# A decoder layer on one core: GpSimd's sums moved to VectorE, bias and memory loaded from the weights' queue, query copies made by DMA

## The chip, the core and the metric

The kernel runs on one core of one Trainium2 chip. The metric is device time in microseconds (us). Engines are named as in the profile: PE is TensorE (PEld its weight loads), DVE is VectorE, ACT is ScalarE, POOL is GpSimd, SP is SyncE, which computes nothing here and issues transfers.

## What is computed

One layer over 256 tokens of width 1024, all in float32: RMSNorm, a combined projection, two self-attention mixers (8 heads of MoBA attention, which with 256 tokens is plain causal attention, and 4 heads of differential attention), then cross-attention to 256 memory tokens, a SwiGLU and a final RMSNorm.

```python
h = rms_norm(x, mix_norm_g)
proj = h @ w_in                        # qa, ka, va, qb, kb, vb
oa = moba_attention(qa, ka, va, table_a)            # softmax(q k / 8 + bias) v, causal
ob = diff_attention(qb, kb, vb, table_b, lam, ...)  # (softmax_0 - lam * softmax_1) v
x = x + concat(rms_norm(oa), rms_norm(ob)) @ w_out
m = rms_norm(mem, mem_norm_g)
x = x + cross_attention(rms_norm(x) @ w_cq, m @ w_ck, m @ w_cv) @ w_co
x = x + (silu(rms_norm(x) @ w_gate) * (rms_norm(x) @ w_up)) @ w_down
return rms_norm(x)
```

## The kernel before

**Weights.** All weights pass as a stream of 65 chunks of 1 MB (`wdma`, L112, SP's queue, three buffers `wr`). Each chunk is converted in four parts (`wpart`): ACT writes the rounded high part `wh` (L135), DVE subtracts it to get the low part `wl` (L120). The subtraction of a part is put into DVE's stream only when the next part is recorded (`held`, `wflush`). A product then takes three matmuls, high x high, high x low, low x high: one step of `ws` (L276) is six matmuls of 256 columns over one k tile and two output tiles, one step of `as_` (L298) three of 512 columns.

**Order.** Each engine runs its own stream in order. The streams are written by a hand-made clock of slots: `run` calls `tick` after each PE step, `at(slot, fn)` and `later(n, fn)` put other work between two steps. A weight part is recorded about every second slot. In slots: chunk 1 (keys `ka0`) to 16, `qa1` to 24, `ka1` to 32, values `v_chunk(0)` to 48, `qb0` to 56, `kb0` to 64, `qb1` to 72, `kb1` to 80, `v_chunk(1)` to 96, then the memory's keys from w_ck.

**The opening.** x comes in five transfers, interleaved on SP's queue with the first weight chunk. `x_gain` multiplies by the norm's gain, `wf` (L342) multiplies the first chunk in plain float32 without a split, `x_split` makes the two halves of h (L267, L268), `squares` squares x on ACT (L324) and adds the squares up on POOL (L326). `x_rstd` sums over partitions by matmul (L333), takes the power on POOL (L246); `x_row` (L253) makes the row RX of it, which `qk_evac` (L372, L375) needs.

**Queries and keys.** A chunk holds four heads of 64 lanes. `q_high` writes the rounded queries twice per half of the partitions (L383, four ACT instructions per chunk: own half and the other), so that keys can stand with their high part in one half and their low part in the other (`k_high` L395 on ACT, `k_low` L400 on DVE; `q_low` is L389). `logits` (L435, L436) runs 4 slots apart for the first mixer, `p_t` (L458) transposes the exponentials six slots later. For the second mixer `diff_mix` (L480) joins two heads before its `p_t`.

**Memory tokens.** `mem_load` brings them by POOL's queue; `mem_squares` (ACT, sums on POOL L326), `mem_rstd`, `mem_row`, `mem_scale` (POOL, L572), `mem_split` (`split_g`: gain and rounding on ACT L261, subtraction on DVE L263).

Of the kernel before, what the change touches and what calls it, by code (L numbers as in the profile page):

```python
# [17 lines left out]
P = 128  # L18
# [44 lines left out]
def layer(ctx: ExitStack, tc: tile.TileContext, xt_d, stream, memT, gains, bias_d, diff_lambda, final_norm_g,  # L63
# [124 lines left out]
    for lo, hi in ((0, 1), (1, 2), (2, 4), (4, 6), (6, 8)):  # L188
        nc.sync.dma_start(xT[:, lo:hi], xt_d[:, lo:hi])
        (nc.sync if lo else nc.scalar).dma_start(w0[:, lo:hi], src[:, lo:hi])  # L190
# [33 lines left out]
    def lambda_dma():  # L224
        nc.gpsimd.dma_start(lp.rearrange("p a b -> p (a b)"),
                            bass.AP(tensor=diff_lambda.tensor, offset=diff_lambda.offset,
                                    ap=[[0, P], [1, 256]]))

    def bias_load(h0, n):
        t = mx.tile([P, n, 256], FT, name="bias", tag="bias", bufs=2)  # L230
        for h in range(n):
            bias[h0 + h] = t[:, h, :]
        nc.gpsimd.dma_start(t, bias_d[:, h0:h0 + n, :])
# [87 lines left out]
    def squares(sqt, src, j):  # L321

        ks = slice(2 * j, 2 * j + 2)
        nc.scalar.activation(sqt[:, ks, :], src[:, ks, :], AF.Square)  # L324
        if j:
            nc.gpsimd.tensor_tensor(sqt[:, 0:2, :], sqt[:, 0:2, :], sqt[:, ks, :], op=OP.add)  # L326
# [229 lines left out]
    def mem_load():  # L556
        nc.gpsimd.dma_start(memv, memT)
# [25 lines left out]
    at(14, x_row)  # L583
    at(46, load_lambda)
    at(10, bias_load, 0, 4)
    at(18, lambda_dma)
    at(20, bias_load, 4, 4)
    at(32, mem_load)
    at(45, bias_load, 8, 4)
    for i in range(8):  # L590
        at(28 + 4 * i, logits, i, i, f"qa{i // 4}", f"ka{i // 4}", i // 2 % 2, i % 2)
        at(34 + 4 * i, p_t, i)
        at((51, 52, 53, 54, 56, 59, 63, 67)[i], pv, i, 0, "a", 64)
    for j in range(4):
# [27 lines left out]
    for j in range(4):
        at((108, 112, 124, 127)[j], mix_t, j)
# [383 lines left out]
```

## Time and profile before

| what | value |
|---|---|
| time, median of 3 runs | 428.75 us (427.72 to 429.9) |
| the profiled execution | 430.01 us, span of its instructions 427.8 us |
| busy in the span | PE 97%, DVE 69%, ACT 59%, POOL 7% |
| moved by DMA | 74 MB, 173 GB/s in the mean |
| mean granted clock of TensorE | 0.994 of full speed |

The page's shares are means over the span: they don't tell the stages apart. A busy PE is not PE at its peak, since the ends of matmuls are modelled; a stage is read from its waits and from the start times of successive matmuls.

### The profile page before, as it was taken

Reading aid. Unit: us, or ns where it says so; the run is one execution under the profiler, and the core shown is the slowest. Engines: PE = TensorE matmul, PEld = TensorE weight load, DVE = VectorE, ACT = ScalarE, POOL = GpSimd, SP = SyncE. Lnnn points to the kernel's source line nnn. Section 1 sums busy time; section 2 is a strip of 40 time slices with the busy share of each in tenths; the row PEclk is TensorE's granted clock in tenths of the full one; section 3 lists DMA queues with packets and bytes.
Section 4 is the critical chain, followed back from the end, with each engine's and each line's share of the span. In section 5 each row is a group of like instructions: output and inputs, shape, how many; then the busy total and the mean of one; then the engine's idle time right before and its main releaser. Section 6 shows DMA issues by size and latency. Waiting matters only on the chain.

```text
span 427.8 us, 6928 instructions
## 1 busy us (share of the span) xinstructions
PE 414.5 (97%) x2677; PEld 375.0 (88%) x2677; DVE 294.0 (69%) x591; ACT 253.4 (59%) x542; POOL 27.9 (7%) x36
## 2 busy tenths in 40 slices
PE   7979999979999999999999999999999999999994
PEld 4879899969998889998888999999888888888883
DVE  3677747989568589476759868888776666544423
ACT  5568869598576555366546565556656655433322
POOL 3500035100010000000000100000000000000001
PEclk9989999999999999999999999999999999999999
DMA  7984552235527534434442555545753575555002
GB/s 225 378 296 161 190 193 100 98 98 199 198 100 278 191 113 144 161 107 190 137 159 98 198 213 186 184 159 205 286 196 110 196 284 198 196 193 190 11 2 98
DMA packets 13040, 73.99 MB, mean 173 GB/s; under 512 B 1584, under 2 KB 2864, under 8 KB 4944
## 3 DMA queue, kind: packets, MB, share of 16 engines
q1 hardware_dynamic: 11664, 69.74, 46.0%
q0 software_dynamic: 768, 3.28, 2.1%
q10 hardware_dynamic: 576, 0.54, 0.4%
q8 instruction: 21, 0.34, 0.3%
q14 instruction: 11, 0.09, 0.1%
HBM read 72.50 MB, written 1.05 MB: 172 GB/s over the span
## 4 chain that ended last, share of the span: by engine, by line
PE 86%; DVE 7%; ACT 3%; issue 2%; DMA 1%; POOL 0%; SPq 0%; POOLq 0%; DVEq 0%; ACTq 0%
PE acc L276 24%; PE y L298 13%; PE acc L298 9%; PE acc L284 9%; PE att L284 9%; PE att L276 5%; PE att L285 4%; PE acc L285 4%; DVE wl L120 2%; PE att L765 1%; PE oc L809 1%; DVE b L263 1%; ACT qs L383 1%; DMA xT<-in_xT_dram 1%; PE att L458 1%
## 5 line engine op out<-in xcount | busy, mean ns | idle before, releaser
L120 DVE TENSOR_TENSOR wl<-wr,wh 128x512 fp32r<-128x512 f32 x255 | 164.5, 691 | 36.0 <-ACT wh L135 35.8
L135 ACT ACTIVATE wh<-wr 128x512 fp32r<-128x512 f32 x255 | 144.1, 620 | 51.1 <-issue 22.6
L276 PE MATMUL acc<-b,wh 128*128 128x256 f32 x536 | 101.2, 289 | 0.0
L276 PEld LDWEIGHTS acc<-b,wh 128*128 128x128 f32 x536 | 84.4, 194 | 0.2
L276 PE MATMUL acc<-b,wl 128*128 128x256 f32 x268 | 76.7, 286 | 2.8 <-DVE wl L120 2.6
L276 PEld LDWEIGHTS acc<-b,wl 128*128 128x128 f32 x268 | 51.9, 194 | 3.2 <-DVE wl L120 3.2
L298 PE MATMUL y<-wh,b 128*128 128x512 f32 x152 | 49.0, 391 | 0.0
L298 PE MATMUL acc<-wh,b 128*128 128x512 f32 x128 | 40.5, 397 | 0.0
L284 PE MATMUL acc<-hs,wh 128*128 128x512 f32 x96 | 37.8, 393 | 0.0
L284 PE MATMUL att<-hs,wh 128*128 128x512 f32 x96 | 37.8, 393 | 0.0
L298 PE MATMUL y<-wl,b 128*128 128x512 f32 x88 | 34.2, 389 | 0.0
L298 PEld LDWEIGHTS y<-wh,b 128*128 128x128 f32 x152 | 28.5, 188 | 5.9
L285 PE MATMUL att<-hs,wl 128*128 128x256 f32 x96 | 27.2, 283 | 0.0
L285 PE MATMUL acc<-hs,wl 128*128 128x256 f32 x96 | 27.1, 283 | 0.0
L298 PEld LDWEIGHTS acc<-wh,b 128*128 128x128 f32 x128 | 22.6, 189 | 3.6
L298 PE MATMUL acc<-wl,b 128*128 128x512 f32 x64 | 25.1, 392 | 0.0
L276 PE MATMUL acc<-cHL,wh 128*128 128x256 f32 x128 | 23.3, 283 | 0.0
L276 PE MATMUL att<-b,wh 128*128 128x256 f32 x128 | 23.2, 283 | 0.0
L284 PEld LDWEIGHTS att<-hs,wh 128*128 128x128 f32 x96 | 18.0, 188 | 4.2
L284 PEld LDWEIGHTS acc<-hs,wh 128*128 128x128 f32 x96 | 18.0, 188 | 4.1
L276 PEld LDWEIGHTS att<-b,wh 128*128 128x128 f32 x128 | 20.0, 192 | 0.0
L450 ACT ACTIVATE e<-e,nm 128x128 f32<-128x128 f32 (+1 forms) x32 | 14.3, 447 | 9.5 <-DVE nm L441 9.5
(206 smaller groups left out, 723.5 us busy)
## 6 DMA issues: line engine op xcount, KB each, us to landing
wr<-in_stream_dram SPq DMA_DIRECT2D x62, 1024.0 KB, 4.8
wr<-in_stream_dram SPq DMA_DIRECT2D x7, 256.0 KB, 6.2
bias<-in_bias_dram POOLq DMA_DIRECT2D x3, 512.0 KB, 5.6
wr<-in_stream_dram SPq DMA_DIRECT2D x2, 512.0 KB, 7.1
b<-in_memT_dram POOLq DMA_DIRECT2D x1, 1024.0 KB, 8.3
xT<-in_xT_dram SPq DMA_DIRECT2D x3, 256.0 KB, 5.3
gfin<-in_final_norm_g_dram POOLq DMA_DIRECT2D x1, 512.0 KB, 6.0
out_dram<-z ACTq DMA_DIRECT2D x2, 192.0 KB, 2.0
```

Of the source, the lines that this page charges most:

```text
L120: eng.tensor_tensor(l, t, h, op=OP.subtract)
L135: nc.scalar.activation(h, t, AF.Copy)
L263: nc.vector.scalar_tensor_tensor(dL[:, k, :], srcs[:, a, :], g(gi + k), dH[:, k, :], op0=OP.mult, op1=OP.subtract)
L276: nc.tensor.matmul(o[:, c, :], m[:, k, cs], b[:, k, :], start=first and c == 0 and q == 0, stop=last and q == 2, skip_group_check=True)
L284: nc.tensor.matmul(o[c], h[:, k, cs], flat(a[:, k]), start=first, stop=last, skip_group_check=True)
L285: nc.tensor.matmul(o[c][:, 0:256], l[:, k, cs], a[:, k, 0, :], start=False, stop=last, skip_group_check=True)
L298: nc.tensor.matmul(o, m[:, ka, ts], b[:, kw, cs], start=start and q == 0, stop=stop and q == 2, skip_group_check=True)
L383: nc.scalar.activation(qs[to, :, r, :], d[half(r)], AF.Copy)
L450: nc.scalar.activation(e[:, cs], e[:, cs], AF.Exp, bias=nm[:, t:t + 1], scale=-1.0, accum_out=lsum[:, i, t:t + 1])
L458: nc.tensor.transpose(b[:, q * P:(q + 1) * P], e[:, q * P:(q + 1) * P], ident)
L765: nc.tensor.matmul(b[:, t, :], a[:, kt, t * P:(t + 1) * P], k[:, kt, :], start=n == 0, stop=n == 5)
L809: nc.tensor.matmul(o[:, dv, :], v[:, mt, cs], p_[:, mt, :], start=n == 0, stop=n == 5)
```

## The change

Sums and products leave POOL: `squares` only squares, `add_squares` adds on DVE; `mem_scale` becomes one DVE instruction per k tile that takes the gain along, and `mem_split` splits without gain. `q_high` makes two ACT copies per chunk, and the other two are transfers inside SBUF, issued by POOL (L387 of the changed kernel). The bias table, lambda and the memory tokens are loaded from SP's queue, behind weight chunks. The gain of x is taken by DVE for six k tiles instead of four; the third and fourth k tile of x and of the first weights come in transfers of their own. Slots move: RX by one, the evacuation of `qa0` by two and of `ka0` by three, the first mixer's attention by two, the memory's norm by three, the second mixer's last four logits by two and its `p_t` by three or four.

```diff
-    for lo, hi in ((0, 1), (1, 2), (2, 4), (4, 6), (6, 8)):
+    for lo, hi in ((0, 1), (1, 2), (2, 3), (3, 4), (4, 6), (6, 8)):
         nc.sync.dma_start(xT[:, lo:hi], xt_d[:, lo:hi])
...
     def lambda_dma():
-        nc.gpsimd.dma_start(lp.rearrange("p a b -> p (a b)"),
+        nc.sync.dma_start(lp.rearrange("p a b -> p (a b)"),
...
-        nc.gpsimd.dma_start(t, bias_d[:, h0:h0 + n, :])
+        nc.sync.dma_start(t, bias_d[:, h0:h0 + n, :])
...
     def x_gain(k):
-        if k % 2:
+        if k % 4:
             nc.vector.tensor_scalar(hF[:, k, :], xT[:, k, :], g(G_MIX + k), None, op0=OP.mult)
...
     def squares(sqt, src, j):
         ks = slice(2 * j, 2 * j + 2)
         nc.scalar.activation(sqt[:, ks, :], src[:, ks, :], AF.Square)
+    def add_squares(sqt, j):
+        ks = slice(2 * j, 2 * j + 2)
         if j:
-            nc.gpsimd.tensor_tensor(sqt[:, 0:2, :], sqt[:, 0:2, :], sqt[:, ks, :], op=OP.add)
+            nc.vector.tensor_tensor(sqt[:, 0:2, :], sqt[:, 0:2, :], sqt[:, ks, :], op=OP.add)
...
     def q_high(name, d):
         qs = mx.tile([P, 2, 2, 256], FR, name="qs", tag="qs", bufs=2)
         for r in range(2):
-            for to in (half(r), half(1 - r)):
-                nc.scalar.activation(qs[to, :, r, :], d[half(r)], AF.Copy)
+            nc.scalar.activation(qs[half(r), :, r, :], d[half(r)], AF.Copy)
+        for r in range(2):
+            nc.gpsimd.dma_start(qs[half(1 - r), :, r, :], qs[half(r), :, r, :])
...
     def mem_load():
-        nc.gpsimd.dma_start(memv, memT)
+        nc.sync.dma_start(memv, memT)
...
     def mem_squares(j):
         squares(mq, memv, j)
+        later(1, add_squares, mq, j)
...
-    def mem_scale(j):
-        t = memv[:, 2 * j:2 * j + 2, :]
-        nc.gpsimd.tensor_tensor(t, t, M["R"].to_broadcast([P, 2, 256]), op=OP.mult)
+    def mem_scale(k):
+        nc.vector.scalar_tensor_tensor(memv[:, k, :], memv[:, k, :], g(G_MEM + k), M["R"][:, 0, :], op0=OP.mult,
+                                       op1=OP.mult)
...
-        split_g(*m, j, memv[:, 2 * j:2 * j + 2, :], G_MEM)
+        ks = slice(2 * j, 2 * j + 2)
+        split(m[0][:, ks, :], m[1][:, ks, :], memv[:, ks, :])
...
-    at(14, x_row)
+    at(15, x_row)
...
-    at(18, lambda_dma)
-    at(20, bias_load, 4, 4)
-    at(32, mem_load)
-    at(45, bias_load, 8, 4)
+    at(26, lambda_dma)
+    at(28, bias_load, 4, 4)
+    at(38, mem_load)
+    at(47, bias_load, 8, 4)
...
-        at(28 + 4 * i, logits, i, i, f"qa{i // 4}", f"ka{i // 4}", i // 2 % 2, i % 2)
+        at(30 + 4 * i, logits, i, i, f"qa{i // 4}", f"ka{i // 4}", i // 2 % 2, i % 2)
...
-    at(59, mem_rstd)
-    at(62, mem_row)
+    at(62, mem_rstd)
+    at(64, mem_row)
...
-        at((73, 75, 77, 79, 88, 90, 92, 94)[i], logits, 8 + i, 8 + i // 2, f"qb{i // 4}", f"kb{i // 4}", i // 2 % 2,
+        at((73, 75, 77, 79, 90, 92, 94, 96)[i], logits, 8 + i, 8 + i // 2, f"qb{i // 4}", f"kb{i // 4}", i // 2 % 2,
...
-        at((78, 82, 93, 97)[hd], diff_mix, hd)
-        at((84, 88, 99, 101)[hd], p_t, 8 + 2 * hd)
+        at((79, 84, 96, 100)[hd], diff_mix, hd)
+        at((88, 92, 102, 104)[hd], p_t, 8 + 2 * hd)
...
-    later(7, qk_evac, o, "qa0", True)
+    later(9, qk_evac, o, "qa0", True)
...
-    later(1, qk_evac, o1, "ka0", False)
+    later(4, qk_evac, o1, "ka0", False)
```

Three places in the streams. Line numbers of the changed kernel are up to 14 higher. First DVE from the evacuation of `qa0` to the evacuation of `qa1`: `qa`, `ka` are evacuated projections, `wl` the low parts of weights, 64x2x256 the low parts of queries (`b<-qa,qs`) and keys. Before:

```order
L372 SCALAR_TENSOR_TENSOR qa_252<-acc,RX 128x512
L120 TENSOR_TENSOR wl<-wr,wh 128x512 x3
L389 TENSOR_TENSOR b_122<-qa_252,qs 64x2x256 x2
L375 TENSOR_TENSOR ka_281<-acc,RX 128x512
L400 TENSOR_TENSOR b_129<-ka_281,b_129 64x2x256 x2
L120 TENSOR_TENSOR wl<-wr,wh 128x512 x4
```

and changed:

```order
L375 SCALAR_TENSOR_TENSOR qa_274<-acc,RX 128x512
L393 TENSOR_TENSOR b_124<-qa_274,qs 64x2x256 x2
L120 TENSOR_TENSOR wl<-wr,wh 128x512
L378 TENSOR_TENSOR ka_306<-acc,RX 128x512
L120 TENSOR_TENSOR wl<-wr,wh 128x512
L404 TENSOR_TENSOR b_131<-ka_306,b_131 64x2x256 x2
L120 TENSOR_TENSOR wl<-wr,wh 128x512 x2
L375 SCALAR_TENSOR_TENSOR qa_350<-acc,RX 128x512
```

Four instructions on queries and keys stood in a row between the third and the fourth `wl` of the row behind `qa`; now a `wl` stands between the queries' two, the evacuation of `ka` and the keys' two.

Second POOL, behind its memsets. The first 12 rows before (`b_126`, `b_137` are squares, `b_136` the memory tokens):

```order
L326 TENSOR_TENSOR b_126<-b_126 128x512 x3
L233 DMA bias<-in_bias_dram 128x1024
L246 TENSOR_TENSOR rx<-rxv,mhalf 128x2
L225 DMA lp<-in_diff_lambda_dram 128x256
L233 DMA bias<-in_bias_dram 128x1024
L557 DMA b_136<-in_memT_dram 128x2048
L233 DMA bias<-in_bias_dram 128x1024
L326 TENSOR_TENSOR b_137<-b_137 128x512 x3
L246 TENSOR_TENSOR rm<-rmv,mhalf 128x2
L572 TENSOR_TENSOR b_136<-b_136,RM 128x512 x4
L246 TENSOR_TENSOR ra<-rav,mhalf 128x2
L246 TENSOR_TENSOR rb<-rbv,mhalf 128x8
```

and all that is left of them in the changed kernel:

```order
L246 TENSOR_TENSOR rx<-rxv,mhalf 128x2
L387 DMA qs<-qs 64x2x256 x6
L246 TENSOR_TENSOR rm<-rmv,mhalf 128x2
L387 DMA qs<-qs 64x2x256 x2
L246 TENSOR_TENSOR ra<-rav,mhalf 128x2
L246 TENSOR_TENSOR rb<-rbv,mhalf 128x8
```

The adds and products are gone, the loads too, and eight transfers of `qs` stand there, two per chunk of queries.

Third DVE from the evacuation of `kb0` to the second mixer's first logits (`b_136` and `b_138` are the memory tokens). Before:

```order
L375 TENSOR_TENSOR kb_835<-acc,RX 128x512
L120 TENSOR_TENSOR wl<-wr,wh 128x512
L263 SCALAR_TENSOR_TENSOR b_846<-b_136,gT,b_845 128x256 x2
L120 TENSOR_TENSOR wl<-wr,wh 128x512
L400 TENSOR_TENSOR b_129<-kb_835,b_129 64x2x256 x2
L263 SCALAR_TENSOR_TENSOR b_846<-b_136,gT,b_845 128x256 x2
L120 TENSOR_TENSOR wl<-wr,wh 128x512
L263 SCALAR_TENSOR_TENSOR b_846<-b_136,gT,b_845 128x256 x2
L120 TENSOR_TENSOR wl<-wr,wh 128x512
L263 SCALAR_TENSOR_TENSOR b_846<-b_136,gT,b_845 128x256 x2
L120 TENSOR_TENSOR wl<-wr,wh 128x512
```

and changed, from the first scaling on:

```order
L576 SCALAR_TENSOR_TENSOR b_138<-b_138,gT,RM 128x256 x2
L378 TENSOR_TENSOR kb_835<-acc,RX 128x512
L120 TENSOR_TENSOR wl<-wr,wh 128x512
L576 SCALAR_TENSOR_TENSOR b_138<-b_138,gT,RM 128x256 x2
L268 TENSOR_TENSOR b_848<-b_138,b_847 128x512
L120 TENSOR_TENSOR wl<-wr,wh 128x512
L576 SCALAR_TENSOR_TENSOR b_138<-b_138,gT,RM 128x256 x2
L404 TENSOR_TENSOR b_131<-kb_835,b_131 64x2x256 x2
L576 SCALAR_TENSOR_TENSOR b_138<-b_138,gT,RM 128x256 x2
L268 TENSOR_TENSOR b_848<-b_138,b_847 128x512
L120 TENSOR_TENSOR wl<-wr,wh 128x512
L268 TENSOR_TENSOR b_848<-b_138,b_847 128x512
```

Eight scalings (L576) have come in, and each pair of L263 has become one L268.

## Rows read from the trace of the kernel before

**Rows 1.** Part 1 of the page: busy time of each engine, share of the span, instructions.
```profile
PE 414.5 (97%) x2677; PEld 375.0 (88%) x2677; DVE 294.0 (69%) x591; ACT 253.4 (59%) x542; POOL 27.9 (7%) x36
```

**Rows 2.** Three stretches in the view of windows: the stretch and its length, then busy us (and instructions) of PE, PEld, DVE, ACT and POOL, the granted clock of TensorE as a share of full speed, the DMA engines' share and GB/s.
```profile
27.00:30.00 3.00, 0.60 (x6) 0.40 (x4) 2.18 (x4) 2.56 (x5) 0.00 (x0) 0.98 0.93 358
30.00:33.20 3.20, 2.97 (x14) 2.97 (x15) 2.58 (x5) 1.47 (x3) 0.00 (x0) 0.50 0.19 64
86.00:96.00 10.00, 7.71 (x37) 5.77 (x37) 9.15 (x26) 9.70 (x25) 0.00 (x0) 1.00 0.32 105
```

**Rows 3.** The view of waits, the rows of PE and its weight loads (PEld): who waited for whom, us in total, how often, the longest. The first three rows are of the whole span, the last two of its first 160 us.
```profile
PE acc L276 <- DVE wl L120: 2.6, 1, 2.6
PE att L458 <- DVE e L480: 1.2, 1, 1.2
PE att L435 <- DVE b L400: 1.0, 1, 1.0
...
PEld acc L276 <- DVE wl L120: 3.2, 2, 2.8
PEld pr L253 <- POOL rx L246: 0.3, 1, 0.3
```

**Rows 4.** PE in the timeline, at three restarts: start, us, engine, line, operation, operands, how many; in brackets the idle time before and what ended it.
```profile
30.23 0.58 PE L276 MATMUL acc<-b,wl 128*128 128x256 f32 x1 [2.63 <-DVE wl L120]
...
89.92 0.83 PE L458 MATMUL att<-ident,e 128*128 128x128 f32 x3 [1.19 <-DVE e L480]
...
94.51 0.33 PE L435 MATMUL att<-b,qs 128*128 128x128 f32 x1 [1.03 <-DVE b L400]
```

**Rows 5.** Three pieces of the chain that ended last: start, us, what, how many matmuls.
```profile
30.23 4.22 PE acc L276 x22
...
34.92 2.88 PE acc L276 x24
...
38.26 1.39 PE acc L298 x6
```

**Rows 6.** DVE in the timeline from 21 to 31 us, columns as in Rows 4.
```profile
21.23 1.29 DVE L120 TENSOR_TENSOR wl<-wr,wh 128x512 fp32r<-128x512 f32 x2
24.58 0.69 DVE L120 TENSOR_TENSOR wl<-wr,wh 128x512 fp32r<-128x512 f32 x1 [2.06 <-ACT wh L135]
25.19 1.38 DVE L389 TENSOR_TENSOR b<-qa,qs 64x512 fp32r<-64x512 f32 x2
26.61 0.69 DVE L375 TENSOR_TENSOR ka<-acc,RX 128x512 f32<-128x512 f32 x1
28.05 1.40 DVE L400 TENSOR_TENSOR b<-ka,b 64x512 fp32r<-64x512 f32 x2 [0.76 <-ACT b L395]
29.49 1.29 DVE L120 TENSOR_TENSOR wl<-wr,wh 128x512 fp32r<-128x512 f32 x2
```

**Rows 7.** ACT in the timeline over the same stretch.
```profile
21.35 2.56 ACT L383 ACTIVATE qs<-qa 64x512 fp32r<-64x512 f32 x4 [0.24 <-DVE qa L372]
23.92 1.15 ACT L135 ACTIVATE wh<-wr 128x512 fp32r<-128x512 f32 x2
27.39 1.28 ACT L395 ACTIVATE b<-ka 64x512 fp32r<-64x512 f32 x2 [2.32 <-DVE ka L375]
28.70 2.19 ACT L135 ACTIVATE wh<-wr 128x512 fp32r<-128x512 f32 x4
```

**Rows 8.** The opening in the timeline: one row of PE, two of DVE, one of POOL.
```profile
7.85 7.64 PE L342 MATMUL acc<-b,wr 128*128 128x256 f32 x32 [0.47 <-DMA wr<-in_stream_dram]
...
6.51 0.35 DVE L313 TENSOR_SCALAR b<-xT,gT 128x256 f32<-128x256 f32 x1
...
8.41 1.36 DVE L313 TENSOR_SCALAR b<-xT,gT 128x256 f32<-128x256 f32 x1
...
8.36 1.26 POOL L326 TENSOR_TENSOR b<-b 128x512 f32<-128x512 f32 x1 [4.59 <-ACT b L324]
```

**Rows 9.** The memory tokens and the second mixer in the timeline: one row of POOL, four of DVE, one of ACT.
```profile
70.53 5.68 POOL L572 TENSOR_TENSOR b<-b,RM 128x512 f32<-128x512 f32 x4 [1.90 <-ACT RM L255]
...
73.54 2.95 DVE L263 SCALAR_TENSOR_TENSOR b<-b,gT,b 128x256 fp32r<-128x256 f32 x2
...
79.96 0.87 DVE L263 SCALAR_TENSOR_TENSOR b<-b,gT,b 128x256 fp32r<-128x256 f32 x2
...
89.51 0.75 DVE L480 SCALAR_TENSOR_TENSOR e<-e,rl 128x128 f32<-128x128 f32 x2
...
93.77 1.41 DVE L400 TENSOR_TENSOR b<-kb,b 64x512 fp32r<-64x512 f32 x2
...
84.02 2.58 ACT L383 ACTIVATE qs<-qb 64x512 fp32r<-64x512 f32 x4
```

**Rows 10.** What a transfer costs: a DMA that POOL issues, and DVE at that time (timeline); then three rows of the view of transfers: tensors, queue, how many, KB each, median us from issue to landing.
```profile
46.37 0.54 POOL L233 DMA_DIRECT2D bias<-in_bias_dram  x1 [25.06 <-DVE nm L441]
...
45.99 0.69 DVE L120 TENSOR_TENSOR wl<-wr,wh 128x512 fp32r<-128x512 f32 x1
...
b<-in_memT_dram POOLq DMA_DIRECT2D x1, 1024.0 KB, 8.3
out_dram<-z SPq DMA_DIRECT2D x2, 128.0 KB, 1.9
lp<-in_diff_lambda_dram POOLq DMA_DIRECT2D x1, 128.0 KB, 5.5
```

More of the change, by code (lines that the diff above doesn't have):

```diff
@@ L224, in lambda_dma @@
     def lambda_dma():
-        nc.gpsimd.dma_start(lp.rearrange("p a b -> p (a b)"),
-                            bass.AP(tensor=diff_lambda.tensor, offset=diff_lambda.offset,
-                                    ap=[[0, P], [1, 256]]))
+        nc.sync.dma_start(lp.rearrange("p a b -> p (a b)"),
+                          bass.AP(tensor=diff_lambda.tensor, offset=diff_lambda.offset,
+                                  ap=[[0, P], [1, 256]]))
     def bias_load(h0, n):
@@ L578, in mem_split @@
             m.extend((slot(4), slot(5)))
-        split_g(*m, j, memv[:, 2 * j:2 * j + 2, :], G_MEM)
+        ks = slice(2 * j, 2 * j + 2)
+        split(m[0][:, ks, :], m[1][:, ks, :], memv[:, ks, :])
     at(12, x_rstd)
-    at(14, x_row)
+    at(15, x_row)
     at(46, load_lambda)
     at(10, bias_load, 0, 4)
-    at(18, lambda_dma)
-    at(20, bias_load, 4, 4)
-    at(32, mem_load)
-    at(45, bias_load, 8, 4)
+    at(26, lambda_dma)
+    at(28, bias_load, 4, 4)
+    at(38, mem_load)
+    at(47, bias_load, 8, 4)
     for i in range(8):
-        at(28 + 4 * i, logits, i, i, f"qa{i // 4}", f"ka{i // 4}", i // 2 % 2, i % 2)
-        at(34 + 4 * i, p_t, i)
-        at((51, 52, 53, 54, 56, 59, 63, 67)[i], pv, i, 0, "a", 64)
+        at(30 + 4 * i, logits, i, i, f"qa{i // 4}", f"ka{i // 4}", i // 2 % 2, i % 2)
+        at(36 + 4 * i, p_t, i)
+        at((53, 54, 55, 56, 58, 61, 65, 69)[i], pv, i, 0, "a", 64)
     for j in range(4):
-        at(52 + j, mem_squares, j)
-    at(59, mem_rstd)
-    at(62, mem_row)
+        at(57 + j, mem_squares, j)
+    at(62, mem_rstd)
+    at(64, mem_row)
+    for k in range(KT):
+        at(65 + k // 2, mem_scale, k)
     for j in range(4):
-        at(63, mem_scale, j)
         at((66, 68, 70, 72)[j], mem_split, j)
@@ L614, in layer @@
     for hd in range(4):
-        at((78, 82, 93, 97)[hd], diff_mix, hd)
-        at((84, 88, 99, 101)[hd], p_t, 8 + 2 * hd)
-        at((104, 105, 106, 107)[hd], pv, 8 + 2 * hd, 1, "b", P)
+        at((79, 84, 96, 100)[hd], diff_mix, hd)
+        at((88, 92, 102, 104)[hd], p_t, 8 + 2 * hd)
+        at((105, 106, 107, 108)[hd], pv, 8 + 2 * hd, 1, "b", P)
     for t in range(2):
-        at(110 + t, diff_stats, t)
-    at(113, diff_rstd)
-    at(118, diff_scale)
+        at(111 + t, diff_stats, t)
+    at(114, diff_rstd)
+    at(119, diff_scale)
     for j in range(4):
-        at((108, 112, 124, 127)[j], mix_t, j)
+        at((109, 113, 125, 128)[j], mix_t, j)
     o = acc()
@@ L628, in layer @@
     state["use"], state["done"], state["slot"] = 2, 1, 8
+    for k in range(4):
+        x_gain(k)
+        wf(o, w0, k)
     for j in range(4):
-        for k in (2 * j, 2 * j + 1):
-            x_gain(k)
-            wf(o, w0, k)
+        if j >= 2:
+            for k in (2 * j, 2 * j + 1):
+                x_gain(k)
+                wf(o, w0, k)
+            add_squares(sqt, j - 1)
         x_split(j)
@@ L647, in layer @@
         wflush()
+        if q == 0:
+            add_squares(sqt, 3)
     run(ws_steps(o1, ready[1], h, range(2, KT)))
-    later(1, qk_evac, o1, "ka0", False)
+    later(4, qk_evac, o1, "ka0", False)
     qk_chunk("qa1", True)
```

## The prediction

> **What bounds the kernel now.** I read the page's busy times first: PE 97%, DVE 69%, ACT 59%, POOL 7% [rows 1]. The kernel is bound by PE, so the question is where PE stands still or runs slowly, and whether the change reaches those places. The view of windows and the waits of PE answer it [rows 2, 3]; the reader is to see that the lost time lies in three short stretches of the first 100 us.
>
> First the opening. PE starts its second pair of k tiles at 7.85 after 0.47 us of waiting for weights and then runs 32 matmuls almost without a break [rows 8]; behind them two short waits follow, for the first low part of weights (3.2 less the long wait of 2.8 = 0.4 us) and for RX's power on POOL (0.3 us) [rows 3].
>
> Second the queries and keys. From 27 to 30 us PE is busy for 0.60 of 3 us [rows 2]; the wait is 2.63 us for one `wl` [rows 4]. The timelines of DVE and ACT tell why it is late [rows 6, 7]. ACT makes four query copies from 21.35 to 23.91 and only then a `wh`; DVE idles 2.06 us for it. Then DVE has the queries' low parts (1.38), the evacuation of `ka` (0.69) and, after 0.76 us for ACT, the keys' low parts (1.40) in a row, and the `wl` that PE wants starts at 29.49. Right behind the pause the granted clock is 0.50, that is 1.2 GHz, until 33.2 [rows 2]: 22 matmuls take 4.22 us where 24 take 2.88 (0.120 each) afterwards [rows 5]. At the full clock they would take 2.64, so 1.6 us go there.
>
> Third the second mixer. From 86 to 96 PE idles 2.3 us [rows 2], 1.19 for the mixed exponentials and 1.03 for the keys' low parts [rows 4], both on DVE, which is busy for 9.15 of the 10 us. DVE came late because POOL scaled the memory tokens from 70.53 to 76.21: two L263 beside it took 2.95 us, the same two later 0.87 [rows 9]. The chain then runs through four more query copies, 2.58 us on ACT [rows 9].
>
> **The change, part by part.** *Opening.* A gain on DVE takes 0.35 us alone and 1.36 beside a POOL sum [rows 8]. Two of them shrink, but PE is busy from 7.85 on, so most of these 2 us are hidden by its own matmuls. PE gains what it starts earlier. The third k tile of weights has its own transfer of half the size, so the 0.47 wait should go, and k tiles 6 and 7 are scaled sooner; then the landing of the next pair limits it. I take 0.65, with 0.4 and 0.3 for the two short waits: 1.4 us. Below, 0.3, if two more issues on SP delay x as much as the smaller pieces help; above, 1.7, with the whole 2 us pulling. The adds on DVE (priced like L268 and `wl`, 0.69 each) lie beside PE's matmuls; without that cover they cost 2.
>
> *Queries and keys.* The sum rests on this walk, with PE ahead by the opening's gain. A chunk is eight steps of 0.72 us (six matmuls at 0.120, [rows 5]). `qa1` then starts near 19.8, `ka1` near 25.6. DVE evacuates `qa0` at 21.3, ACT makes two copies instead of four (0.64 each [rows 7]), ending at 23.2. DVE does the queries' low parts until 24.0, and now a `wl` comes before `ka`: it is done at 24.6, one microsecond before PE wants it. `ka` is evacuated by 25.3, the second `wl` done at 25.9 (wanted 27.0), the keys' low parts at 27.4, the third `wl` at 28.0 (wanted 28.4), the fourth at 28.6 (wanted 29.9). So the wait goes, 2.7 us (2.63 on PE, 2.8 on its weight load [rows 3, 4]), and with it the slow clock, 1.6. The thinnest margin is 0.4 us. What becomes late next is the third `wl`, behind the keys.
>
> *Query copies by DMA.* POOL issues one in about 0.54 us [rows 10]. No row shows a copy inside SBUF. The nearest is `lp`, 128 KB by POOL's queue, 5.5 us to landing under a loaded queue; the smallest is 1.9 us for 128 KB on SP, the longest 8.3 us for 1 MB [rows 10]. The first copy is released at 22.6 and the first logits, two slots later than before, want it at 29.9: 7.3 us of room. For the second mixer it is released at 85.3 on the old time axis (84.02 and two copies, [rows 9]) and wanted at 93.3: PE's restart at 94.51 less its waits of 1.03 and 1.19 [rows 4], and some 1.0 for two slots more without the transposes that moved behind them. That is 8.0 us of room. I take 5.5, which costs nothing; 8.3 would cost 1.0 and 0.3.
>
> POOL's issue could also be held off by DVE. A row speaks against that: an issue at 46.37 took 0.54 us while DVE ran a `wl` from 45.99 to 46.68 [rows 10], and that `wl` took its usual 0.69. The Trainium skill, page "SBUF — State Buffer", section "SBUF: two separate sides", warns of exactly this: while DVE holds the port pair it shares with GpSimd, GpSimd can't write descriptors and its DMA seems to hang behind DVE; it names two-port modes as the holders, and the instructions around these copies are subtractions with two inputs. If the subtractions held it too, the time would be that of the last rival below; by the row it is nothing.
>
> *Loads on SP's queue.* Bias, lambda and memory now stand behind weight chunks. The first bias is issued right behind chunk 3, as early as before; the second behind chunk 6, near 29, and lands by 37 with 8.3 us; the logits that need it run near 41. The memory tokens stand behind chunk 7 and land some 10 us before their squares. Cost nothing; what a weight chunk loses is the transfer in front of it, 1 to 3 us of a queue that runs far ahead of PE there.
>
> *Memory and second mixer.* DVE gets eight scalings of 0.44 (half of 0.87 [rows 9]), 3.5 us. It loses the blocked 2.1 (2.95 less 0.87) and 0.7 (four L268 of 0.69 for four pairs of 0.87), the waits behind the two missing copies (about 0.9 of their 1.3), and one `diff_mix` of 1.1 moves behind the keys. Net it is 1.3 us earlier at the keys of `kb1`. PE wants them two slots later, 1.4 us (a slot of L298 is 1.39/2 = 0.7 [rows 5]); the exponentials of the first pair four slots later, 2.8. Against a lateness of 2.3 to 3 that leaves 0.3. The memory's norm gets one slot less between `mem_rstd` and `mem_row`, with POOL's power and DVE's copy between them: I take 0.4 lost (0 to 0.8). So 2.3 - 0.3 - 0.4 = 1.6, between 0.5 and 2.8.
>
> *Sum.* 1.4 + 2.7 + 1.6 + 1.6 = 7.3 us. The profiled execution took 430.0, which gives 422.7; it stands 1.3 above the median, so against 428.75 it is 421.5.
>
> **The rivals.**
> *DVE stays the bound at the keys.* The adds and the evacuations are all on DVE now, and the thinnest margin is 0.4 us. If DVE is later by 2 us, PE waits about 1.6 for the third `wl`, and the clock may fall again (1.6). Against it: DVE idled 2.06 + 0.76 there. Time 421.5 + 3.2 = 424.7.
> *The second mixer's waits stay.* DVE was busy for 9.15 of 10 us and gets 3.5 more. If only the first two stages gain, it is 428.75 - 5.7 = 423.0; if the added work comes on top, 425.
> *It changes little.* If ACT's copies were not what held the `wl` and the stall only moves to `v_chunk(0)`, the opening's 1.4 is left: 427.3, within 0.5%. Rows 6 speak against it, since DVE's wait names `wh`.
> *Copies land late, slower.* If POOL's issue waits for a gap on DVE, against the row of 46.37 [rows 10], the first pair is issued when DVE's row ends at 28.6 and lands at 34.1: PE waits 4.2 at the first logits, and 1.6 of slow clock follow. At the second mixer DVE is without a gap until 93.8 [rows 9], landing 99.3, wanted 93.3: 6.0 and 1.6. Together 13.4: 434.9. It decides from a landing 9.7 us after release: waits of 2.4 and 1.7 and twice 1.6 then eat the 7.3. The mechanism is that of the page of the Trainium skill named above ("SBUF — State Buffer"), with subtractions as holders.
>
> **How the numbers follow.** Chances: forecast 0.68 (own range 419 to 423.5), DVE at the keys 0.12, second mixer 0.08, little 0.06, late copies 0.06. Within 0.5% (426.6 to 430.9) is about what a measurement of this kernel can't tell from no change. Faster by more takes the first three and is 0.88; same 0.06; slower 0.06. The range is from all terms at their upper bound (1.7 + 2.8 + 1.6 + 2.8 = 8.9, and 1 for the spread of runs), 418.9, to DVE bound in both places, 426: it leaves out about 0.14.
>
> **What would show it.** Right: no wait of PE above 0.5 us between 20 and 35, and a granted clock of 1.00 there; the gains of x at 0.35 us each; `v_chunk(0)` starting near 32 instead of 38.3 [rows 5]; waits of PE at L462 and L439 of the second mixer below 0.5 together. Wrong: PE waiting for a copy of `qs` (a DMA named as releaser), a clock of 0.50 anywhere before the end, DVE busy without a gap from 21 to 35, or a wait at the memory's row L253 of over 1 us.

## The result, and the profile after

The changed kernel takes 426.4 us (median; 424.83 to 427.96) against 429.32 (427.72 to 431.54) for the kernel before, measured in turn: a ratio of 0.9927, 95% interval 0.9907 to 0.9947. The gain is 0.7%, about 3 us; the forecast was 421.5, with a range of 418.9 to 426.0. So the direction was right and the size was not: more than half of the sum is missing. The profiled execution of the changed kernel took 427.14 us, its span 425.4, against 430.01 and 427.8 before. The kernel before does not fall to the lower clock in every execution: of 33 measured beside the experiments, 13 had a mean granted clock of 0.998 or 0.999 and took 428.54 to 428.92 us, and 20 had 0.991 to 0.995, as the profiled one (0.994), and took 428.97 to 430.96.

Part 1 of the page after the change, which answers to [rows 1]:

```profile
PE 414.3 (97%) x2677; PEld 375.4 (88%) x2677; DVE 294.8 (69%) x603; ACT 246.4 (58%) x528; POOL 16.5 (4%) x29
```

POOL lost 11 us of work and ACT 7; PE's busy share is unchanged. The view of windows shows the three stretches of [rows 2] and a new one from 68 us on (columns as there):

```profile
27.00:30.00 3.00, 3.00 (x28) 3.00 (x26) 2.81 (x5) 1.57 (x3) 0.17 (x1) 1.00 0.92 293
30.00:33.20 3.20, 3.20 (x29) 3.20 (x28) 2.47 (x5) 2.13 (x5) 0.00 (x0) 1.00 0.18 22
...
68.00:71.40 3.40, 3.40 (x19) 3.40 (x18) 0.71 (x2) 0.63 (x2) 1.10 (x1) 0.51 0.84 308
86.00:96.00 10.00, 10.00 (x53) 8.44 (x52) 9.67 (x28) 8.66 (x24) 0.00 (x0) 1.00 0.52 155
```

The places that the change was expected to mend are mended. From 27 to 30 us PE is busy for 3.00 of 3 us (0.60 before), the granted clock behind it is 1.00 (0.50 before), and from 86 to 96 PE has no idle time (2.29 us before), although DVE is busier than before. What is new stands in the middle: from 68 to 71.4 the granted clock is 0.51, the lower of its two levels, at a place where the kernel before ran at full speed.

The view of waits, PE's rows of the first 110 us (who waited for whom, us in total, times, longest; left out is the warm-up ahead of the first product), against [rows 3]:

```profile
PE acc L345 <- DMA wr<-in_stream_dram: 2.7, 3, 1.4
...
PE att L336 <- DVE b L329: 1.0, 1, 1.0
```

PE's waits for `wl`, for the mixed exponentials and for the keys' low parts are all gone. Two others have come: the opening's matmuls (L345, the L342 of before) wait for the first weight chunk, and the memory's sum over partitions (L336) waits for DVE's sums of squares.

The opening in the timeline (start, us, engine, line, operation, operands, how many; in brackets the idle time before and what ended it), first of the kernel before, PE's first split product:

```profile
15.14 0.58 PE L276 MATMUL acc<-b,wh 128*128 128x256 f32 x2
```

then PE of the changed kernel, up to the same product:

```profile
4.82 4.57 PE L345 MATMUL acc<-b,wr 128*128 128x256 f32 x16 [0.43 <-DMA wr<-in_stream_dram]
10.30 1.97 PE L345 MATMUL acc<-b,wr 128*128 128x256 f32 x8 [0.92 <-DMA wr<-in_stream_dram]
13.62 3.69 PE L345 MATMUL acc<-b,wr 128*128 128x256 f32 x16 [1.35 <-DMA wr<-in_stream_dram]
16.96 0.59 PE L276 MATMUL acc<-b,wh 128*128 128x256 f32 x2
```

Before, 32 matmuls ran from 7.85 almost without a break [rows 8]. Now the wait of 0.47 us at 7.85 is gone, as forecast, but PE waits at 10.30 for k tiles 4 and 5 and at 13.62 for 6 and 7, and the first split product starts 1.8 us later than before. The forecast had it 0.65 us earlier, and put the other 0.7 us of its 1.4 behind it. DVE is not the cause: the gains of x take 0.35 us each, as foretold. The chain that ended last up to 20 us shows the transfer that PE waits for at 13.62 (issue, us to landing):

```profile
5.86 7.62 DMA wr<-in_stream_dram
```

These are the last two k tiles of the first weights. Before, they were issued at 4.77 and landed 6.1 us later, at 10.86; now they are issued at 5.86 and land at 13.48. Of the 2.6 us, 1.1 are the later issue and 1.5 the longer way from issue to landing.

The two short waits behind the first split product are gone, too. The product that opens `qa1` starts 1.1 us later than before, not 1.8; first the kernel before, then the changed one:

```profile
21.44 0.40 PE L276 MATMUL acc<-b,wh 128*128 128x256 f32 x2
```

```profile
22.56 0.40 PE L276 MATMUL acc<-b,wh 128*128 128x256 f32 x2
```

One thing is not named under the change: the changed kernel also puts the gains and the products of the first four k tiles ahead of the first splits of x. No run parts this order from the rest.

The memory's norm, the same timeline of PE, DVE and ACT:

```profile
66.69 1.02 PE L336 MATMUL att<-ones,b 128*128 128x2 f32 x8 [0.96 <-DVE b L329]
...
65.06 1.48 DVE L329 TENSOR_TENSOR b<-b 128x512 f32<-128x512 f32 x2
...
71.62 0.88 DVE L576 SCALAR_TENSOR_TENSOR b<-b,gT,RM 128x256 f32<-128x256 f32 x2 [2.90 <-ACT RM L255]
...
64.88 0.62 ACT L323 ACTIVATE b<-b 128x512 f32<-128x512 f32 x1
```

The last square (ACT L323) runs from 64.88; the last two sums on DVE (L329) start at 65.06 and end at 66.54; PE, which is ready for L336 at 65.7, idles 0.96 us. The clock falls some 1.3 us after L336 starts. DVE then idles 2.90 us for the row RM, which comes out of matmuls that run at the lower clock.

The query copies, two transfers of 128 KB per chunk, cost POOL and the queue this (last line of the view of the tile `qs` up to 110 us, then POOL and DVE in the timeline at one pair):

```profile
DMA to landing us min/median/max: 2.3/3.3/7.4
...
62.18 1.23 POOL L387 DMA_DIRECT2D qs<-qs  x2 [27.61 <-ACT qs L385]
...
62.46 0.69 DVE L329 TENSOR_TENSOR b<-b 128x512 f32<-128x512 f32 x1
```

The median from issue to landing is 3.3 us, the longest 7.4, and PE never waits for one. The longest belongs to the second pair, issued from 33.34 on, right after SP had issued a weight chunk, lambda and a bias table; it landed by 41.2, and its first logits ran at 47.0.

### The profile page after: what moved, and what is told of

It is laid out like the page before. It is cut to its first block, busy times and chain, and to the rows that moved or that the text cites. A ratio compares the mean times of both kernels' runs of the same rounds, so it can differ in the third digit from the quotient of the medians.

```text
span 425.4 us, 6946 instructions
## 1 busy us (share of the span) xinstructions
PE 414.3 (97%) x2677; PEld 375.4 (88%) x2677; DVE 294.8 (69%) x603; ACT 246.4 (58%) x528; POOL 16.5 (4%) x29
## 4 chain that ended last, share of the span: by engine, by line
PE 90%; DVE 3%; DMA 3%; issue 2%; ACT 1%; SPq 0%; POOLq 0%; POOL 0%; DVEq 0%; ACTq 0%
PE acc L276 25%; PE y L298 13%; PE acc L298 10%; PE acc L284 9%; PE att L284 9%; PE att L276 5%; PE att L285 5%; PE acc L285 5%; DMA wr<-in_stream_dram 2%; PE att L779 1%; PE oc L823 1%; DVE wl L120 1%; PE att L462 1%; PE att L439 1%; PE acc L345 1%
## 5 line engine op out<-in xcount | busy, mean ns | idle before, releaser
L298 PEld LDWEIGHTS acc<-wh,b 128*128 128x128 f32 x128 | 22.6, 188 | 3.6
L298 PEld LDWEIGHTS y<-wl,b 128*128 128x128 f32 x88 | 16.6, 189 | 3.6
```

Of the source, the lines that this page charges most:

```text
L298: nc.tensor.matmul(o, m[:, ka, ts], b[:, kw, cs], start=start and q == 0, stop=stop and q == 2, skip_group_check=True)
```

## The experiments

Ratios are against the kernel before in the same series of runs.

**Five transfer pairs in the opening again.** The changed kernel with

```diff
-    for lo, hi in ((0, 1), (1, 2), (2, 3), (3, 4), (4, 6), (6, 8)):
+    for lo, hi in ((0, 1), (1, 2), (2, 4), (4, 6), (6, 8)):
```

> The changed kernel with x and the first weights in five pairs of transfers again, as before the change; all else is kept. In the changed kernel the last piece of the first weights landed at 13.5 us instead of 10.9 and the first split product started at 16.96 instead of 15.14. Theory: the two additional pairs of small transfers slow the opening. Then the last piece lands near 10.9, the split products start between 14.0 and 15.1, and the time falls by 1.8 to 3 us against the changed kernel (426.4), to about 424. Rival: the late landing has another cause (the adds on DVE, an idle POOL, this one execution); then the split products still start near 17 and the time stays within 0.7 us of the changed kernel.

424.08 us, 0.9879 [0.9846, 0.9912]. PE in the opening:

```profile
7.83 7.14 PE L345 MATMUL acc<-b,wr 128*128 128x256 f32 x32 [1.05 <-DVE b L268]
14.63 0.59 PE L276 MATMUL acc<-b,wh 128*128 128x256 f32 x2
```

The two new stops are gone and the split product starts 2.3 us earlier than in the changed kernel, within what the theory gave; by the ratios the six pairs cost 2.1 us (0.9927 less 0.9879, of 429). The stall at L336 and the lower clock behind it stayed, so they do not come from the opening.

**The memory's squares earlier.** The changed kernel with

```diff
-        at(57 + j, mem_squares, j)
+        at(52 + j, mem_squares, j)
```

> The changed kernel with the squares of the memory tokens recorded at slots 52 to 55 as before the change, instead of 57 to 60; the adds follow one slot later each. In the changed kernel PE waits 1.0 us for the last add at 66.7, does eight matmuls of two columns, and the granted clock is 0.5 from 68.0 to 71.5. Theory: the late adds cost this wait and the slow clock behind it, 1.1 + 1.7 us; then both go, the granted clock stays 1.00 up to the end of the program, and the time falls by 2.5 to 3.2 us to about 423.5. Rival: the stage is bound by DVE and ACT as a whole and the loss moves on to the scalings or to the second mixer; then waits of PE of 1 us or more appear between 70 and 95 and the time falls by less than 1 us.

424.82 us, 0.9896 [0.9853, 0.9939]. PE's waits in the first 110 us, again without the warm-up:

```profile
PE acc L345 <- DMA wr<-in_stream_dram: 1.6, 2, 1.0
...
PE att L439 <- DVE nm L445: 0.3, 1, 0.3
```

The wait at L336 is gone, the clock is not lowered anywhere before the end, and the span is 422.7, 2.7 less than that of the changed kernel. The ratios give it only 1.3 us (0.9927 less 0.9896), under what the theory had, and their intervals overlap: the time alone does not tell the cost from nothing, the rows do. In the executions profiled the slow stretch goes with the wait. Why the ratios show less than the two profiled executions was not found.

**Both.** The two edits together.

> Both of these together: five pairs of transfers in the opening, squares of the memory tokens at slots 52 to 55. If the two losses are independent the time falls by the sum of the two runs, about 5 us, to 421 to 422. If the PE only catches up with the next late engine, by less: then a new wait of 1 us or more stands in the profile between 20 and 100 us.

422.71 us, 0.9844 [0.9818, 0.9871], span 421.1. This is faster than both kernels, and it is what the change gives without its two faults: 6.7 us (5.5 to 7.8). The two repairs add up: 3.6 us by the ratios together, 2.1 and 1.3 singly. PE's first split product and its first of `v_chunk(0)`:

```profile
15.00 0.59 PE L276 MATMUL acc<-b,wh 128*128 128x256 f32 x2
...
32.57 0.63 PE L298 MATMUL acc<-wh,b 128*128 128x512 f32 x2
```

**Copies on ACT.** The changed kernel with the four ACT copies of before, its order kept:

```diff
-            nc.scalar.activation(qs[half(r), :, r, :], d[half(r)], AF.Copy)
-        for r in range(2):
-            nc.gpsimd.dma_start(qs[half(1 - r), :, r, :], qs[half(r), :, r, :])
+            for to in (half(r), half(1 - r)):
+                nc.scalar.activation(qs[to, :, r, :], d[half(r)], AF.Copy)
```

> The changed kernel with all four query copies of a chunk on ACT again and no transfers inside SBUF; order and slots as changed. Theory of the prediction: the two copies fewer on ACT are part of what removes the wait of 2.7 us near 30 us; with four copies ACT is later by 1.3 us per chunk, PE waits 0.5 to 1.5 us between 25 and 40, and the time rises by 0.5 to 3 us (the upper end with the slow clock behind it). Rival: the order alone, a low part of weights between the low parts of queries and the evacuation of keys, removes the wait; then PE has no wait above 0.5 us between 25 and 40 and the time stays within 0.7 us of the changed kernel.

429.44 us, 1.0004 [0.9986, 1.0022]. Waits of PE, and the clock in its opening (windows):

```profile
PE acc L345 <- DMA wr<-in_stream_dram: 2.9, 2, 2.5
PE att L336 <- DVE b L329: 1.9, 1, 1.9
...
PE acc L298 <- DVE wl L120: 0.8, 1, 0.8
...
PE acc L276 <- DVE wl L120: 0.2, 1, 0.2
```

```profile
11.00:14.40 3.40, 3.40 (x9) 2.68 (x10) 1.70 (x4) 1.15 (x2) 0.00 (x0) 0.50 1.01 337
```

The transfers are worth 3 us in the changed order. But the long wait at the keys does not return with the ACT copies: only 0.2 and 0.8 us do. The copies make themselves felt at L336 (1.9 instead of 1.0 us) and in the second mixer, where PE waits 0.5 and 0.2 us at its logits (L438). Part of the loss in the profiled execution is a lowered clock in the opening, where no copy runs, so this run alone doesn't price them. The next two part the two causes.

**The transfers alone.** The kernel before with the same edit the other way round: two ACT copies, two transfers, nothing moved.

> The kernel before with one edit: half of the query copies are transfers inside SBUF, nothing is moved. Theory (ACT's four copies held the wh, and so the wl that PE wants): ACT is free 1.3 us earlier, the 2.6 us wait of PE at the keys shrinks to about 1.3 or less; the granted clock behind it may still fall. The waits of 1.2 and 1.0 us in the second mixer shrink by about 1.3 together. Time 424 to 427 us. Rival (the order of the slots made the gain at the keys): the wait stays above 2 us, time 428 to 429.5. A third possibility: without the two later slots the copies land too late for the logits and PE waits for a DMA named qs; time 429 or more.

426.7 us, 0.9928 [0.9903, 0.9953]. PE at the keys and at the second mixer (timeline):

```profile
28.97 0.39 PE L276 MATMUL acc<-b,wl 128*128 128x256 f32 x1 [1.38 <-DVE wl L120]
...
86.55 0.83 PE L459 MATMUL att<-ident,e 128*128 128x128 f32 x3 [0.41 <-DVE e L481]
91.14 0.33 PE L436 MATMUL att<-b,qs 128*128 128x128 f32 x1 [1.03 <-DVE b L401]
```

The wait at the keys shrinks from 2.63 to 1.38, by the two copies of 0.64 that ACT no longer makes, and this time the clock behind it stays at 1.00. In the second mixer the wait for the exponentials falls from 1.19 to 0.41; the one for the keys' low parts stays, so that the two together shrink by 0.8 and not by the 1.3 expected.

**The order alone.** The kernel before with the moves of the first half:

```diff
-    at(14, x_row)
+    at(15, x_row)
...
-        at(28 + 4 * i, logits, ...
-        at(34 + 4 * i, p_t, i)
+        at(30 + 4 * i, logits, ...
+        at(36 + 4 * i, p_t, i)
...
-    later(7, qk_evac, o, "qa0", True)
+    later(9, qk_evac, o, "qa0", True)
...
-    later(1, qk_evac, o1, "ka0", False)
+    later(4, qk_evac, o1, "ka0", False)
```

> The kernel before with the moves of the first half alone: evacuation of qa0 and ka0 later, RX's row one slot later, the first mixer's logits, p_t and p.v two slots later; four copies on ACT as before. Theory drawn from the kernel with ACT copies: the order alone takes most of the wait at the keys, at most 0.4 us of it left and up to 1 us at v_chunk(0), granted clock 1.00 there; time about 425 us (2.6 + 1.6 less 1). Rival (the copies were the cause): the wait of 2.6 us stays and the clock is 0.50 behind it, 428.5 to 429.5.

426.71 us, 0.993 [0.9905, 0.9955]. PE's waits:

```profile
PE att L435 <- DVE b L400: 1.0, 1, 1.0
PE acc L298 <- DVE wl L120: 0.8, 1, 0.8
PE att L458 <- DVE e L480: 0.7, 1, 0.7
...
PE acc L276 <- DVE wl L120: 0.2, 1, 0.2
```

and ACT, which in [rows 7] made the query copies ahead of `wh`:

```profile
20.96 1.66 ACT L135 ACTIVATE wh<-wr 128x512 fp32r<-128x512 f32 x3
23.54 2.58 ACT L383 ACTIVATE qs<-qa 64x512 fp32r<-64x512 f32 x4 [0.92 <-DVE qa L372]
```

The order alone takes 1.6 us of the wait (2.63 to 0.2 and 0.8), and the slow clock with it: three `wh` are ready before ACT turns to the four copies. By the ratio it is worth as much as the transfers alone. The two overlap, since with either of them the clock stays up in the execution profiled.

**Six pairs alone.** The kernel before with the six transfer pairs.

> The kernel before with six transfer pairs in the opening instead of five, nothing else. Theory (two more transfers ahead of the last weights delay them by about 2.5 us): w6:8 lands at 13 instead of 10.9 us, ws starts at 17.0 to 17.5 instead of 15.1, time 430.5 to 431.5, ratio 1.004 to 1.006. Rival (it costs only together with the loads on SP and the adds on DVE): ws starts near 15, time 428.5 to 429.5, ratio 1.00.

430.57 us, 1.0026 [1.0005, 1.0047]. PE in the opening:

```profile
12.36 3.69 PE L342 MATMUL acc<-b,wr 128*128 128x256 f32 x16 [0.93 <-DMA wr<-in_stream_dram]
15.70 0.59 PE L276 MATMUL acc<-b,wh 128*128 128x256 f32 x2
```

and, from the chain that ended last, the transfer of the last two k tiles of weights:

```profile
5.68 6.54 DMA wr<-in_stream_dram
```

The edit is a loss here too: 1.1 us by the ratio, where the six pairs cost 2.1 in the changed kernel, and 0.6 by the split product. The intervals do not tell the two costs apart. The time lies where the theory had it, the ratio and the split product lie between theory and rival. The last weights land at 12.22, 1.4 us later than before: 0.9 by the later issue, 0.5 by the way from issue to landing. The view of windows from 8 to 13 us shows the rate (last column, GB/s); first before, then this kernel, then the changed one:

```profile
8.00:13.00 5.00, 4.97 (x22) 3.80 (x23) 3.82 (x4) 2.59 (x6) 2.54 (x2) 1.00 1.00 339
```

```profile
8.00:13.00 5.00, 4.07 (x19) 3.13 (x18) 3.31 (x4) 2.70 (x6) 2.54 (x2) 1.00 0.98 304
```

```profile
8.00:13.00 5.00, 3.35 (x15) 2.32 (x13) 3.80 (x8) 2.89 (x6) 0.00 (x0) 1.00 0.95 242
```

The DMA engines are busy throughout (0.95 to 1.00), but with six pairs they move 304 and 242 GB/s where it was 339. Why six pairs lower it more in the changed kernel than here was not found; each row comes from one execution.

**Weights issued on ACT.** The changed kernel with the earlier squares and

```diff
-        (nc.sync if lo else nc.scalar).dma_start(w0[:, lo:hi], src[:, lo:hi])
+        nc.scalar.dma_start(w0[:, lo:hi], src[:, lo:hi])
```

> The changed kernel with the memory's squares at slots 52 to 55 and with all weights of the opening issued on ACT instead of SP; six transfer pairs as in the change. Theory 1 (the issues in a row, 0.47 us each with a wait for the transfer eight before, hold back the last weights): w6:8 is issued near 4.7 instead of 5.9 us and lands by 11, ws starts near 15, time about 422.7, ratio 0.984. Theory 2 (the smaller rows of 1 KB move more slowly, whoever issues them): w6:8 lands at 13 as now, ws starts near 16.8, time about 424.8, ratio 0.990.

426.95 us, 0.9934 [0.9908, 0.996]; both theories missed. Behind the issues ACT's own gain of x was late, and PE with it:

```profile
8.41 11.56 PE L345 MATMUL acc<-b,wr 128*128 128x256 f32 x40 [4.02 <-ACT b L315]
```

ACT brought a delay of its own. Nor did the edit bring the issue forward, as the first theory wanted: the six issues of weights took ACT until 6.43 us, the last two k tiles were issued at 6.10 and landed at 13.26. So this run doesn't part the theories. By the landings in the other two kernels both count: the later issue with 0.9 and 1.1 us, the way to landing with 0.5 and 1.5. Whether the second part comes from the smaller rows stays open.

**Back to the parts of before, one at a time**, all on the kernel with both repairs (0.9844), in a series of its own. First the sums of squares on POOL:

```diff
-            nc.vector.tensor_tensor(sqt[:, 0:2, :], sqt[:, 0:2, :], sqt[:, ks, :], op=OP.add)
+            nc.gpsimd.tensor_tensor(sqt[:, 0:2, :], sqt[:, 0:2, :], sqt[:, ks, :], op=OP.add)
```

> The changed kernel with five transfer pairs in the opening and the memory's squares at slots 52 to 55, and the sums of squares (of x and of the memory tokens) on POOL again instead of DVE. Theory (the gains of x beside a POOL sum take 1.36 instead of 0.35 us, but PE's own matmuls hide them, as the prediction said): ws starts at 15.0 to 15.4, time 422.7 to 423.5, ratio 0.984 to 0.987. Rival (the blocked gains hold PE back by the better part of 2 us): ws starts at 16 to 17, time 424 to 425.

424.16 us, 0.987 [0.9847, 0.9893]. PE, then DVE:

```profile
12.83 3.72 PE L345 MATMUL acc<-b,wr 128*128 128x256 f32 x16 [1.66 <-DVE b L313]
16.20 0.59 PE L276 MATMUL acc<-b,wh 128*128 128x256 f32 x2
...
8.53 1.45 DVE L313 TENSOR_SCALAR b<-xT,gT 128x256 f32<-128x256 f32 x1
```

A gain beside a POOL sum takes 1.45 us again, PE waits 1.66 for one, and the split product starts 1.2 us later than in the base, whose opening is otherwise the same. In the five executions profiled with five pairs and the sums on DVE it starts between 14.35 and 15.55. So the rival holds by the trace: with six of the eight gains on DVE, PE's matmuls do not hide the ones that POOL blocks; in the kernel before, with four, they did [rows 8]. The ratio is 0.0026 above the base, 1.1 us.

Then the scaling of the memory tokens on POOL, as `mem_scale` and `split_g` did it before, at slot 65:

> The same base, with the memory tokens scaled by POOL in four instructions at slot 65 as before the change (the gain of the norm back in the splits). Theory (POOL beside DVE holds two of DVE's instructions for 2.1 us, and DVE is then late in the second mixer): DVE loses about 2 us near 70 to 75, waits of PE of 0.5 to 1.5 us return at 85 to 98, time 423.2 to 424.2, ratio 0.986 to 0.989. Rival (the moved maps have room for it): no wait above 0.5 us there, time 422.7, ratio 0.984.

423.5 us, 0.986 [0.9825, 0.9895]. POOL, DVE, then PE:

```profile
67.29 5.40 POOL L577 TENSOR_TENSOR b<-b,RM 128x512 f32<-128x512 f32 x4 [1.15 <-ACT RM L255]
...
69.15 2.38 DVE L263 SCALAR_TENSOR_TENSOR b<-b,gT,b 128x256 fp32r<-128x256 f32 x2 [1.73 <-ACT b L261]
71.45 1.79 DVE L120 TENSOR_TENSOR wl<-wr,wh 128x512 fp32r<-128x512 f32 x1
...
88.82 0.33 PE L439 MATMUL att<-b,qs 128*128 128x128 f32 x1 [0.32 <-DVE b L404]
93.75 0.33 PE L439 MATMUL att<-b,qs 128*128 128x128 f32 x1 [0.53 <-DVE nm L445]
```

DVE loses 2.6 us beside POOL (2.38 instead of 0.87 [rows 9], 1.79 instead of 0.69), and PE waits 0.85 instead of 0.3. The Trainium skill, page "SBUF — State Buffer", section "SBUF: two separate sides", says that a DVE instruction with two inputs in SBUF and a POOL instruction that reads SBUF exclude one another; these rows agree.

Then the second mixer at the slots of before, with the repairs and all else of the change:

```diff
-        at((73, 75, 77, 79, 90, 92, 94, 96)[i], logits, ...
+        at((73, 75, 77, 79, 88, 90, 92, 94)[i], logits, ...
...
-        at((79, 84, 96, 100)[hd], diff_mix, hd)
-        at((88, 92, 102, 104)[hd], p_t, 8 + 2 * hd)
+        at((78, 82, 93, 97)[hd], diff_mix, hd)
+        at((84, 88, 99, 101)[hd], p_t, 8 + 2 * hd)
...
```

> The same base, with the second mixer's logits, mixed maps, transposes, p.v and norms at the slots of the kernel before. Theory (the two slots later make up for DVE's eight scalings): waits of PE of together 1.5 to 2.5 us return at the keys' low parts and the mixed exponentials, time 424.2 to 425.2, ratio 0.988 to 0.991. Rival (the copies and the scaling were enough): no wait above 0.5 us, time 422.7, ratio 0.984.

423.76 us, 0.9865 [0.9839, 0.9891]. PE:

```profile
83.71 0.83 PE L462 MATMUL att<-ident,e 128*128 128x128 f32 x3 [0.32 <-DVE e L484]
88.30 0.33 PE L439 MATMUL att<-b,qs 128*128 128x128 f32 x1 [1.02 <-DVE b L404]
```

The waits return with 1.3 us, just under what the theory gave. The later slots are what removes the wait for the keys' low parts, the one that the transfers alone left.

Last, bias, lambda and memory on POOL's queue at their old slots:

> The same base, with the loads of bias, lambda and memory issued by POOL at the slots of the kernel before. Theory (the loads on SP cost and bring nothing, as the prediction took them): same waits of PE, time 422.4 to 423.0, ratio 0.984. Rival (POOL's issue is held off by DVE, or the loads take from the query copies on the same queue): a copy of the queries lands over 7 us after its release and PE waits for it, or the copies land late without a wait; time 423.5 or more.

423.64 us, 0.9859 [0.9835, 0.9883]; the waits behind the opening are the same single 0.3 us, and no copy of queries is waited for. Nor did the copies land late: 4.1 us from issue to landing at the most. The time lies above what both the theory's range and the base give, although no row shows a cost of the loads; the split product happened to start at 15.55 here. The other three stand at most 0.5 us above it, and all four intervals overlap its own, so none of the four costs is told from zero by its time. The rows tell the first three.

## Why the prediction was wrong, point by point

PE's start times price the terms one by one. From the timelines of the profiled executions, in us, parted at the first products of `qa1` and of `v_chunk(1)`:

| stretch of PE | before | changed | both repairs | order alone | transfers alone | forecast for the change |
|---|---|---|---|---|---|---|
| start to `qa1` (the opening) | 21.4 | 22.6 | 20.6 | 21.2 | 21.4 | 1.4 less |
| `qa1` to `v_chunk(1)` (keys, the memory's norm) | 64.4 | 63.3 | 60.6 | 61.7 | 61.8 | 4.3 less, 0.4 more |
| `v_chunk(1)` to the end (second mixer) | 342.0 | 339.5 | 339.9 | 341.6 | 341.7 | 2.0 less |

**Keys' wait and slow clock, 2.7 + 1.6: right in the main.** No wait of PE above 0.5 us remains between 20 and 35, and the clock is 1.00. With the norm repaired, the stretch is 3.8 us shorter, against 4.3. `v_chunk(0)` was to start near 32; it starts at 32.57 once the opening is repaired, and at 34.5 in the changed kernel, by what the opening lost. The reason was half right: the prediction laid the gain on two copies fewer on ACT, and the two runs on the kernel before show that the order, with `wl` ahead of the evacuation of `ka`, does as much alone (2.7 against 2.6 us).

**Copies by DMA, 0: right.** Issues of 0.6 us and a median of 3.3 us to landing, where 5.5 were taken and 7.3 and 8.0 allowed. The 5.5 did not hold for every copy: the second pair took 7.2 and 7.4 us. The first pair, whose room was the 7.3, took 4.5 and 4.1 us from issue and landed 2 us ahead of its logits. The rival in which the copies land late did not come about: POOL issued a pair from 62.18 to 63.41 while DVE ran a sum with two inputs from 62.46, at their usual durations. What the Trainium skill, page "SBUF — State Buffer", section "SBUF: two separate sides", says of holders in a two-port mode was not put to the test: the rows don't name an instruction's mode.

**Second mixer, 2.3 - 0.3: right.** PE's idle time from 86 to 96 fell by 2.29 us, the stretch by 2.5 (2.1 with both repairs) against 2.0, and the single experiments name the two means: transfers for the exponentials, later slots for the keys.

**Opening, +1.4: wrong in sign.** It was the first half of the failure: `qa1` starts 1.1 us later instead of 1.4 earlier. The 0.7 us of the two short waits came; the step that failed is the 0.65 ahead of them, that the smaller transfers bring k tiles 6 and 7 sooner. Instead the first split product is 1.8 us late, because the last weights land 2.6 us later. The lower bound of 0.3 ("two more issues on SP delay x as much as the smaller pieces help") left out that these weights could also take longer from issue to landing, 7.6 us instead of 6.1; no row of before showed single k tiles against pairs under load, and I took the sign for granted. With five pairs the sign is right: in five executions `qa1` starts 0.3 to 1.5 us earlier than the 21.44 of before, 0.9 in the mean. The two short waits make 0.7 of that, so the shorter gains bring little more. Taking the sums off POOL is worth something all the same: in the new order they would cost 1.2 at this product.

**The memory's norm, -0.4: the second half.** The step counted the slot lost between `mem_rstd` and `mem_row`. It overlooked the distance ahead of it: the squares moved by five slots and the sum over partitions by three, so that two slots less lie between the last square and L336, and one of the rest is taken by the adds, which were put a slot behind the squares. The forecast priced DVE's eight scalings; the three sums of the memory's squares that came to DVE too it put at nothing, and it gave them no due time. The loss was 0.96 us of idle time and then a lowered clock, together 2.7 in the profiled executions (63.3 against 60.6 in the table) and 1.3 by the ratios. "A clock of 0.50 anywhere before the end" stood in the list of what would show the prediction wrong; no rival had it at this place.

**The sum.** Without these two terms the forecast's own terms give 4.3 + 2.0 = 6.3 us. The kernel with both repairs gains 6.7 (5.5 to 7.8). The opening takes 2.1 of it and the norm 1.3, which leaves 3.3; measured were 3.1. One step of the sum itself was loose: the 1.6 us of slow clock come from a profiled execution that had it (430.0), and many executions of the kernel before do not, so the whole sum could not be taken off the median of 428.75. Taken off the profiled execution it gives 422.7, as the prediction also says. Of the rivals none was this: 426.4 lies near the time of the one in which little changes (427.3), yet every stall that rival kept is gone, and two that no rival named have come.

## What to carry to other kernels

Where work moves to other slots, write down for each consumer how many slots lie to its last producer, before and after, and not only at the places that the change is about: a sum that moves less than the squares it needs becomes a wait. A smaller first transfer isn't an earlier last one: where PE works almost without a break behind the opening, the landing of the last piece counts. Two remedies for one stall, here the transfers and the order, don't add up, so price each alone.

## What the runs showed of the chip that I had not expected

The length of one pause doesn't tell whether the granted clock falls, and the same program doesn't always have it fall: 13 of 33 executions of the kernel before show, by their mean clock and their time, no stretch at the lower level, though no trace of one of them was kept. It fell behind 0.96 us of idle time and eight matmuls of two columns (L336 in the changed kernel). In the run with ACT copies the same place had 1.92 us of idle time and the clock stayed at 1.00:

```profile
68.00:71.40 3.40, 1.90 (x16) 1.93 (x17) 2.10 (x5) 1.67 (x4) 0.40 (x1) 1.00 0.25 36
```

There it had already fallen once, in the opening, behind a wait of 2.5 us. It stayed up behind 1.38 us in the kernel with transfers alone, behind 1.19 and 1.03 in [rows 4], and behind 4.02 us in the opening of the kernel with the weights issued on ACT (1.00 from 8 to 22 us).
